# GLA value products in a new order, sums of chunk pairs in PSUM: a two-layer decoder trunk on one core

## The chip, the cores and the metric

The kernel runs on one core of one Trainium2 chip. The metric is the time of one execution in device microseconds (us), the median of several runs. Beside the runs there is one profiled execution, from which all rows below come. Instants in the text are us from the start of its span.

## The reference

A trunk of two layers on 1024 tokens of width 1024, all in fp32. Layer 0 mixes with attention and retention, layer 1 with gated linear attention (GLA, 4 heads, keys of 128, values of 256, chunks of 64 tokens). Behind each mixer stands a gated MLP of width 2816 with a causal convolution of three taps.

```
def odd_mixer(hn, w_in, w_alpha, b_alpha, out_gain, w_out):
    p = hn @ w_in
    g_q, g_k, g_v, g_r, g_a = jnp.split(p, cuts, axis=-1)
    log_alpha = jax.nn.log_sigmoid(g_a @ w_alpha + b_alpha) / GLA_GATE_TAU
    o = gla_chunked(to_heads(g_q), to_heads(g_k), to_heads(g_v), to_heads(log_alpha))
    return (from_heads(rms_norm(o, out_gain)) * jax.nn.silu(g_r)) @ w_out

def conv_ffn(hn, w_up, conv_w, conv_b, w_down):
    u, v = jnp.split(hn @ w_up, 2, axis=-1)
    uc = conv_b + conv_w[0] * up[:, 0:s] + ...        # causal, 3 taps, up is u padded
    return (jax.nn.silu(uc) * v) @ w_down

for layer in range(DEPTH):
    h = h + mixer(rms_norm(h, mix_norm_g[layer]))
    h = h + conv_ffn(rms_norm(h, ffn_norm_g[layer]), ...)
```

## The kernel before

The residual stream h lies in SBUF, transposed: 8 chunks of 128 channels by 1024 tokens. The tokens fall into two halves of 512, t1 and t2 (HALVES). Chunks c and c+4 are a pair (c = 0 to 3).

An fp32 matrix product is made of three matmuls: left and right operand are each split into a rounded part "hi" (made on ScalarE) and the rest "lo" (made on VectorE or GpSimd, as operand minus hi). One left tile times one right tile so costs three matmuls, two of them with the left hi and one with the left lo.

The projections from h work on blocks of two by two (two weight units by two chunk groups, two token halves) with seven products in place of eight, in the order 1, 2, 6, 7, 5, 4, 3. Each product runs over the four pairs, so it has 4 x 3 = 12 matmuls of 512 columns. In GLA's values the roles are turned round: h is the stationary side, and a product has 48 matmuls of 256 columns. The right operands are self.right[c][k], for pair c and product k. Those of products 1, 2 and 3 are "direct": a quarter of h times the norm's gain (ffn_direct, lines L1461 and L1462). Those of 6, 7, 5 and 4 are "mixed": sums of the quarters of h[c] and h[c + 4] (ffn_mixed in the MLPs, with the sums in L1480, L1481, L1482, L1486, L1493 and the splits in L1473 and L1474; gla_mixed in GLA, with L941, L942, L947, L955 and the splits in L927 and L928). For one pair these are five operations on VectorE for the sums and four splits, of which three have their lo on VectorE and that of product 5 on GpSimd. All of their inputs lie in SBUF; in GLA they overwrite h. The factor 1/rms of the norm is not in these operands. It comes in where a product is evicted, so that the squares of h (square_sum, L231) are summed beside the first products and norm_end makes rstd from them by a matmul.

Around the change the work stands so:

- **The end of a mixer's output projection.** The last sums of h (L459, VectorE, one PSUM operand each) come as the banks of the projection (L447 to L449) finish. Beside them VectorE and ScalarE make the right operands of pairs 0 and 1.
- **The first unit of the MLP's up projection** (ffn_up with first given). Product 1 runs over all four pairs and its copy p is taken by ScalarE (L1573); then mid() issues the mixed sums of pairs 2 and 3 and the squares of h[2], h[3], h[6], h[7]; products 2, 6 (copy p2, L1601), 7 (copy p7, L1602), 5, 4, 3 follow.
- **GLA.** gla_values(0) runs the seven products of the first half of the values, beside gla_mixed for pairs 0 and 1, then 2 and 3. Then the norm ends, decay_input makes the input of the decays, and gla_values(1) (the second half of the values) is interleaved with the decays of the heads: decay(h) runs two matmuls per token half (al, L1082) and a chain on VectorE and ScalarE (L1084 to L1102) that ends in the tiles eq and ek. These are kept for head 0 and written to DRAM for heads 1 to 3, to be read back later. gla_qk(h) makes q and k of a head: 84 matmuls (L982 to L984). It stands before the last decay for head 0, and for the others in the loop over heads, ahead of the head's attention. Attention of head 0 begins with gcb (L1179).

A scheduler places the instructions of each engine by priorities and modelled durations, so the order of the code is not the order on the engines; issue_after ties an instruction behind another. Buffers are named by tags: O and st are single PSUM tiles for sums and statistics; pj, z and T are pairs of PSUM tiles; lg and ap are pools in SBUF.

The block that a product runs in the MLP:

```
for c in range(4):
    bh, bl = self.right[c][k]
    nc.tensor.matmul(ps, hi[:, w], bh, ...)
    nc.tensor.matmul(ps, hi[:, w], bl, ...)
    nc.tensor.matmul(ps, lo[:, w], bh, ...)
```

Of the kernel before, what the change touches and what calls it, by code (L numbers as in the profile page):

```python
# [26 lines left out]
class Trunk:  # L27
# [903 lines left out]
    def gla_mixed(self, cs, h, keep=()):  # L931

        nc = self.nc
        t1, t2 = HALVES
        t = {}
        for i, c in enumerate(cs):
            ga, gb = [self.gains[:, 2 * NC + d:2 * NC + d + 1] for d in (c, c + 4)]
            x, y, z = h[c][:, t1], keep[i] if keep else h[c][:, t2], h[c + 4][:, t2]
            t[c] = x, y, z
            nc.vector.tensor_scalar(x, x, ga, None, op0=ALU.mult)  # L940
            nc.vector.scalar_tensor_tensor(y, h[c][:, t2], ga, x, op0=ALU.mult, op1=ALU.subtract)  # L941
            nc.vector.scalar_tensor_tensor(z, z, gb, y, op0=ALU.mult, op1=ALU.subtract)  # L942
            t2_hi = self.t2_hi = self.gla_split(6, c, z, nc.vector)
        yield
        for c in cs:
            x, y, z = t[c]
            nc.vector.tensor_tensor(x, z, x, op=ALU.subtract)  # L947
            self.gla_split(7, c, x, nc.vector)
        for c in cs:
            with self.tc.issue_after(t2_hi):  # L950
                self.gla_split(5, c, t[c][1], nc.gpsimd)
        for c in cs:
            z, w = t[c][2], h[c + 4][:, t1]
            gb = self.gains[:, 2 * NC + c + 4:2 * NC + c + 5]
            nc.vector.scalar_tensor_tensor(w, w, gb, z, op0=ALU.mult, op1=ALU.subtract)  # L955
            self.gla_split(4, c, w, nc.vector)
# [53 lines left out]
    def value_operands(self, hp, s):  # L1010
# [4 lines left out]
        for k, src in (("11", u[0]), ("21", v[0]), ("22", v[1]), ("12", u[1])):  # L1015
            raw[k] = self.load_weight(src[:, cs], 512)[0]
        return self.up_operands(raw, self.wp.tile([P, 512], F32, tag="wr", name="ws", bufs=6))

    def gla_values(self, s, ops, vt):
# [5 lines left out]
        def product(bank, k):  # L1025
            hi, lo = next(ops)
            start = bank not in banks
            if start:
                tag = {"x": "pj", "y": "z", "z": "T"}[bank]
                banks[bank] = [self.psum.tile([P, 512], F32, tag=tag, name="pv", bufs=2) for _ in range(2)]  # L1030
# [174 lines left out]
    def odd_mixer(self, start, dec, outs, res):  # L1205
# [6 lines left out]
        h, first, mixed, keep = start  # L1212
# [36 lines left out]
        for _ in mixed:  # L1249
            pass  # L1250
        for _ in self.gla_values(0, first, v[0]):
# [8 lines left out]
        ops = self.value_operands(0, 1)  # L1260
        ops = itertools.chain([next(ops) for _ in range(1)], ops)
        p1 = pool("gla1")
        fac = [p1.tile([P, NC], F32, name=f"fac{h}") for h in range(4)]
        for _ in self.gla_mixed((2, 3), h):
            pass
# [18 lines left out]
        work = self.gla_values(1, ops, v[0])  # L1284
        e = [None] * 4

        def decay(h):
            e[h] = self.gla_decay(h, ga, dp, fac[h])
            if h > 0:
                for i, t in enumerate(e[h]):  # L1290
                    nc.sync.dma_start(dec[2 * h - 2 + i], t)
# [17 lines left out]
        for h in range(4):  # L1309
            if h > 0:  # L1310
                e[h] = [self.ap.tile([P, T], F32, tag="ac", name="e", bufs=8) for _ in range(2)]
                for i, t in enumerate(e[h]):
                    nc.sync.dma_start(t, dec[2 * h - 2 + i])
# [137 lines left out]


# [11 lines left out]
    def ffn_mixed(self, cs, h, gi, tmp):  # L1464
# [3 lines left out]
        v = nc.vector  # L1468
        t = {}

        def split(c, k, x, engine):
            hi, lo = self.right[c][k] = self.op(self.slot[c, k])
            i = nc.scalar.copy(hi, x)  # L1473
            j = engine.tensor_tensor(lo, x, hi.bitcast(F32), op=ALU.subtract)  # L1474
            return i.ins, j.ins

        for c in cs:
            ga, gb = [self.gains[:, gi * NC + d:gi * NC + d + 1] for d in (c, c + 4)]
            x, y, z = t[c] = tmp(c)
# [573 lines left out]
```

## Time and profile before

| | |
|---|---|
| median of 3 runs | 2425.88 us (2424.42 to 2426.86) |
| the profiled execution | 2428.32 us, span 2426.5 us |
| mean granted clock of TensorE | 0.985 |
| TensorE (PE) busy | 95% of the span, 11672 matmuls |
| VectorE (DVE) busy | 66% |
| ScalarE (ACT) busy | 46% |
| GpSimd (POOL) busy | 60% |

The profiled execution lies 2.4 us above the median. A row of an engine's timeline gives the start in us, the duration, the engine, the line, the operation with out<-in and the tile's shape, how many instructions of the kind stand in a row, and in brackets how long the engine had been idle and what released it. [...] A busy share is an average over stages with different limits, so the stages around the change are read apart.

### The profile page before, as it was taken

What the parts mean: (1) busy time and instruction counts of PE and PEld (TensorE: products, weight loads), DVE (VectorE), ACT (ScalarE), POOL (GpSimd) and SP (SyncE); (2) the same over time, 40 slices, a digit from 0 to 9 for tenths busy, and PEclk for the clock granted to TensorE, in tenths of its full rate; (3) what the DMA queues carried; (4) which work ended last, traced back from release to release, by engine and by line L of the source; (5) the groups of instructions that cost most, each with busy time, mean ns of one, the idle gap of its engine ahead of it and who ended that gap; (6) DMA issues with size and microseconds to landing.
All of it is one profiled execution on the core that took longest, in us unless ns stands there. A gap on an engine that the chain in (4) does not pass through costs nothing. (4 is left out here: it accounts for less than half of the span.)

```text
span 2426.5 us, 33069 instructions
## 1 busy us (share of the span) xinstructions
PE 2310.9 (95%) x11672; PEld 1875.3 (77%) x11672; DVE 1595.9 (66%) x2301; ACT 1114.3 (46%) x2008; POOL 1452.9 (60%) x1098
## 2 busy tenths in 40 slices
PE   8999999998799999999998889998889999999999
PEld 8887886975678888887787668986668888887787
DVE  7667677479976666664339975459986666665234
ACT  6445443244565555552225555355465555553121
POOL 2322323356677777756867645657667777766774
PEclk9999999998999999999999999999999999999999
DMA  4010001112144443459843122232334334339953
GB/s 160 27 36 23 23 23 44 35 53 88 57 152 145 142 156 135 157 196 362 297 163 101 43 100 87 71 113 70 103 98 170 145 141 156 135 139 341 341 202 117
DMA packets 142118, 312.35 MB, mean 129 GB/s; under 512 B 16288, under 2 KB 16672, under 8 KB 141952
## 3 DMA queue, kind: packets, MB, share of 16 engines
q1 hardware_dynamic: 141952, 310.23, 36.5%
q8 instruction: 92, 1.51, 0.3%
q14 instruction: 74, 0.61, 0.1%
HBM read 210.55 MB, written 99.61 MB: 128 GB/s over the span
## 5 line engine op out<-in xcount | busy, mean ns | idle before, releaser
L72 POOL TENSOR_TENSOR wl<-wr,wh 128x512 fp32r<-128x512 f32 x499 | 670.3, 1347 | 460.3 <-ACT wh L70 446.6
L70 ACT CAST wh<-wr 128x512 fp32r<-128x512 f32 x536 | 330.2, 621 | 554.1 <-PE up L1564 194.1
L1563 PE MATMUL up<-op,wh 128*128 128x512 f32 x1232 | 490.3, 398 | 21.4 <-DVE h L459 10.6
L1564 PE MATMUL up<-op,wh 128*128 128x512 f32 x1232 | 489.6, 397 | 2.0 <-DVE op L1474 2.0
L1565 PE MATMUL up<-op,wl 128*128 128x512 f32 x1232 | 488.7, 397 | 0.0
L1712 DVE TENSOR_TENSOR h<-dn,h 128x512 f32<-128x512 f32 x224 | 153.7, 690 | 253.9 <-PE dn L1708 252.5
L1563 PEld LDWEIGHTS up<-op,wh 128*128 128x128 f32 x1232 | 232.6, 189 | 81.4 <-ACT wh L70 11.4
L1564 PEld LDWEIGHTS up<-op,wh 128*128 128x128 f32 x1232 | 232.6, 189 | 59.5 <-DVE op L1474 2.9
L1565 PEld LDWEIGHTS up<-op,wl 128*128 128x128 f32 x1232 | 232.6, 189 | 57.0
L1708 PE MATMUL dn<-op,wl 128*128 128x512 f32 x616 | 244.4, 397 | 5.7 <-POOL wl L72 5.7
L1707 PE MATMUL dn<-op,wh 128*128 128x512 f32 x616 | 244.0, 396 | 0.0
L1706 PE MATMUL dn<-op,wh 128*128 128x512 f32 x616 | 243.0, 396 | 0.0
L161 PE MATMUL pv<-wh,xhi 128*128 128x256 f32 x512 | 153.4, 300 | 1.3 <-ACT xhi L242 1.3
L162 PE MATMUL pv<-wl,xhi 128*128 128x256 f32 x512 | 146.1, 286 | 1.9 <-POOL wl L72 1.0
L163 PE MATMUL pv<-wh,xlo 128*128 128x256 f32 x512 | 145.2, 285 | 1.2 <-DVE xlo L243 1.0
L1708 PEld LDWEIGHTS dn<-op,wl 128*128 128x128 f32 x616 | 115.9, 188 | 35.6 <-POOL wl L72 7.5
L1706 PEld LDWEIGHTS dn<-op,wh 128*128 128x128 f32 x616 | 115.9, 188 | 29.0 <-DVE g L1569 0.4
L1707 PEld LDWEIGHTS dn<-op,wh 128*128 128x128 f32 x616 | 115.8, 188 | 28.2
L585 DVE TENSOR_TENSOR_SCAN r<-r,zeros 128x512 f32<-128x512 f32 (+3 forms) x96 | 104.1, 1086 | 24.6 <-ACT r L578 20.9
L1569 DVE TENSOR_TENSOR up<-up,p 128x512 f32<-128x512 f32 x88 | 61.5, 699 | 87.8 <-PE up L1565 87.8
L447 PE MATMUL out<-op,wh 128*128 128x512 f32 x224 | 91.0, 413 | 16.5 <-ACT op L352 8.7
L161 PEld LDWEIGHTS pv<-wh,xhi 128*128 128x128 f32 x512 | 97.9, 191 | 10.3 <-issue 7.6
(345 smaller groups left out, 5145.2 us busy)
## 6 DMA issues: line engine op xcount, KB each, us to landing
b<-put SPq DMA_DIRECT2D x154, 512.0 KB, 2.7
op<-b SPq DMA_DIRECT2D x308, 256.0 KB, 5.3
wr<-in_wup_dram SPq DMA_DIRECT2D x176, 256.0 KB, 2.6
wr<-in_wdn_dram SPq DMA_DIRECT2D x44, 256.0 KB, 4.1
wr<-in_we_v_dram SPq DMA_DIRECT2D x32, 256.0 KB, 2.8
wr<-in_wod_t_dram SPq DMA_DIRECT2D x32, 256.0 KB, 2.6
wr<-in_we_t_dram SPq DMA_DIRECT2D x24, 256.0 KB, 2.6
a<-in_wdn_dram SPq DMA_DIRECT2D x24, 256.0 KB, 3.9
```

Source lines behind the costliest of these rows:

```text
L70: self.last_hi = nc.scalar.copy(hi, x).ins
L72: self.last_lo = (engine or nc.gpsimd).tensor_tensor(lo, x, hi.bitcast(F32), op=ALU.subtract).ins
L161: nc.tensor.matmul(o, self.xhi[c][:, t], hi[:, w], start=start, stop=False, skip_group_check=True)
L162: nc.tensor.matmul(o, self.xhi[c][:, t], lo[:, w], start=False, stop=False, skip_group_check=True)
L163: nc.tensor.matmul(o, self.xlo[c][:, t], hi[:, w], start=False, stop=(c == NC - 1), skip_group_check=True)
L1563: nc.tensor.matmul(ps, hi[:, w], bh, start=(start and c == 0), stop=False, skip_group_check=True)
L1564: nc.tensor.matmul(ps, hi[:, w], bl, start=False, stop=False, skip_group_check=True)
L1565: nc.tensor.matmul(ps, lo[:, w], bh, start=False, stop=(c == 3), skip_group_check=True)
L1706: nc.tensor.matmul(ps, wh[:, w], gh, start=start, stop=False, skip_group_check=True)
L1707: nc.tensor.matmul(ps, wh[:, w], gl, start=False, stop=False, skip_group_check=True)
L1708: nc.tensor.matmul(ps, wl[:, w], gh, start=False, stop=end, skip_group_check=True)
L1712: nc.vector.tensor_tensor(h[d][:, s], ps, h[d][:, s], op=ALU.add)
```

## The change

It has four parts.

1. **The mixed sums go to PSUM.** A new function sums_psum is used in both places. ScalarE writes minus gain times one quarter of h to a PSUM tile, four operations on VectorE make the sums of products 6, 7, 5 and 4 in two PSUM tiles, and all four lo are made on VectorE. A pair has eight operations on VectorE as before (then five sums and three lo), one more on ScalarE and none on GpSimd. The tiles are O and st (for pair 3 of an MLP two of pj). h is no longer overwritten in GLA. A small constant tile gneg holds the negated gains.
2. **The first unit of an up projection** runs products 1, 2 and 7 over pairs 0 and 1 first (18 matmuls), then product 1 over 2 and 3, and so on; four left operands instead of two are made ahead. The squares of the four later chunks are issued behind copy p7 and no longer with mid().
3. **GLA's values**: products 1 and 2 of both halves (4 x 48 matmuls in place of 2 x 48) come first, in PSUM tiles of their own, and then the rest of the first half beside the mixed sums. Left operands of both halves are made ahead.
4. **GLA's heads**: after the decays of heads 0 and 1 and seven steps of the second half come q and k of head 0, the decay of head 2, q and k of head 1 and the decay of head 3, all ahead of attention. eq and ek of head 1 are not written to DRAM any more.

```
+    def sums_psum(self, x, g, banks, split):
+        nc = self.nc
+        v = nc.vector.scalar_tensor_tensor
+        a, b = banks
+        ga, gn, gb = g
+        nc.scalar.activation(a, x[1], AF.Copy, scale=gn)
+        v(b, x[3], gb, a, op0=ALU.mult, op1=ALU.add)
+        v(a, x[0], ga, b, op0=ALU.mult, op1=ALU.add)
+        yield split(6, a)
+        yield split(7, b)
+        v(b, x[3], gb, a, op0=ALU.mult, op1=ALU.subtract)
+        v(a, x[2], gb, a, op0=ALU.mult, op1=ALU.subtract)
+        split(5, b)
+        yield split(4, a)
...
-    def ffn_mixed(self, cs, h, gi, tmp):
+    def ffn_mixed(self, cs, h, gi, banks):
...
-            v.tensor_scalar(x, h[c][:, t1], ga, None, op0=ALU.mult)
-            v.scalar_tensor_tensor(y, h[c][:, t2], ga, x, op0=ALU.mult, op1=ALU.subtract)
-            v.scalar_tensor_tensor(z, h[c + 4][:, t2], gb, y, op0=ALU.mult, op1=ALU.subtract)
-            split(c, 6, z, v)
...
-            v.tensor_tensor(x, z, x, op=ALU.subtract)
-            split(c, 7, x, v)
...
-            split(c, 5, t[c][1], nc.gpsimd)
...
-            v.scalar_tensor_tensor(z, h[c + 4][:, t1], gb, z, op0=ALU.mult, op1=ALU.subtract)
-            last = split(c, 4, z, v)
...
+            sums.append(self.sums_psum(x, g, banks(c), functools.partial(split, c)))
+        for _ in range(3):
+            last = [next(x) for x in sums][-1]
...
-        x = product("x", 1)
+        late = range(4)
+        if first is not None:
+            late = (2, 3)
+            product("x", 1, (0, 1))
+            product("y", 2, (0, 1))
+            lefts[6] = next(ops)
+            product("z", 7, (0, 1))
+        x = product("x", 1, late)
         nc.scalar.copy(p, x)
         if first is not None:
             mid()
-        y = product("y", 2)
+        y = product("y", 2, late)
...
         nc.scalar.copy(p2, product("x", 6))
-        nc.scalar.copy(p7, product("z", 7))
+        i = nc.scalar.copy(p7, product("z", 7, late))
+        if first is not None:
+            with self.tc.issue_after(i.ins):
+                squares()
...
-        for _ in self.gla_values(0, first, v[0]):
+        works = [self.gla_values(s, firsts[s], v[0], (("pj", "z", "z"), ("T", "z", "z"))[s]) for s in range(2)]
+        for work in works:
+            next(work)
+            next(work)
+        for _ in itertools.chain(*mixed[:2]):
+            pass
+        for _ in itertools.islice(works[0], 2):
+            pass
+        for _ in itertools.chain(*mixed[2:]):
+            pass
+        for _ in works[0]:
             pass
...
-        step(3)
+        step(1)
         decay(0)
-        step(4)
+        step(2)
         decay(1)
-        step(2)
-        decay(2)
         step(7)
         self.gla_qk(0, *e[0], p1, s2())
+        decay(2)
+        self.gla_qk(1, *e[1], p1, s2())
         decay(3)
```

The order on the engines, at three places. VectorE at the end of layer 1's output projection, before (out and h in L459 are the projection's sums, bt the temporary tiles of the mixed sums, op the operands):

```order
L459 TENSOR_TENSOR h<-out,h 128x512
L1493 SCALAR_TENSOR_TENSOR bt<-h,gains,bt 128x512
L1462 SCALAR_TENSOR_TENSOR op<-h,gains,op 128x512 x2
L459 TENSOR_TENSOR h<-out,h 128x512
L1474 TENSOR_TENSOR op<-bt,op 128x512
L1462 SCALAR_TENSOR_TENSOR op<-h,gains,op 128x512 x2
L459 TENSOR_TENSOR h<-out,h 128x512
L1480 TENSOR_SCALAR bt<-h,gains 128x512
L1462 SCALAR_TENSOR_TENSOR op<-h,gains,op 128x512
L459 TENSOR_TENSOR h<-out,h 128x512
```

and after (mx are the PSUM tiles of the sums; L1480 is now the lo of the direct operands, L1490 that of the mixed ones):

```order
L459 TENSOR_TENSOR h<-out,h 128x512
L1465 SCALAR_TENSOR_TENSOR mx<-h,gains,mx 128x512
L1466 SCALAR_TENSOR_TENSOR mx<-h,gains,mx 128x512
L1490 TENSOR_TENSOR op<-mx,op 128x512
L459 TENSOR_TENSOR h<-out,h 128x512
L1490 TENSOR_TENSOR op<-mx,op 128x512
L1480 SCALAR_TENSOR_TENSOR op<-h,gains,op 128x512 x2
L459 TENSOR_TENSOR h<-out,h 128x512
```

The sums of h stand among the same kinds of work, which now read one SBUF tile and one PSUM tile each.

ScalarE in the first unit of layer 1's up projection, before (p is the copy of product 1, p_16556 and p_16557 are p2 and p7, nsq the squares):

```order
L1573 COPY p<-up 128x512
L1473 CAST op<-bt 128x512 x3
L70 CAST wh<-wr 128x512
L1473 CAST op<-bt 128x512
L231 ACTIVATE nsq<-h 128x512 x6
L1601 COPY p_16556<-up 128x512
L231 ACTIVATE nsq<-h 128x512 x2
L1602 COPY p_16557<-up 128x512
L257 CAST shi<-ssum 128x512
```

and after (L1591, L1619 and L1620 are the copies p, p2 and p7):

```order
L1591 COPY p<-up 128x512
L1489 CAST op<-mx 128x512
L70 CAST wh<-wr 128x512 x2
L1489 CAST op<-mx 128x512
L70 CAST wh<-wr 128x512
L1489 CAST op<-mx 128x512
L1619 COPY p_16549<-up 128x512
L1620 COPY p_16550<-up 128x512
L231 ACTIVATE nsq<-h 128x512 x8
L257 CAST shi<-ssum 128x512 x2
```

The copies p2 and p7 moved ahead of all eight squares.

VectorE at the entry of GLA, before (L1712 are the last sums of h, gv the values that are evicted from pv):

```order
L1712 TENSOR_TENSOR h<-dn,h 128x512 x3
L941 SCALAR_TENSOR_TENSOR y<-h,gains 128x512 x2
L942 SCALAR_TENSOR_TENSOR h<-h,gains,y 128x512 x2
L947 TENSOR_TENSOR h<-h 128x512
L928 TENSOR_TENSOR op<-h,op 128x512 x3
L947 TENSOR_TENSOR h<-h 128x512
L955 SCALAR_TENSOR_TENSOR h<-h,gains 128x512 x2
L928 TENSOR_TENSOR op<-h,op 128x512 x3
```

and after:

```order
L1733 TENSOR_TENSOR h<-dn,h 128x512 x3
L1461 SCALAR_TENSOR_TENSOR mx<-h,gains,mx 128x512
L232 TENSOR_TENSOR ssum<-ssum,nsq 128x512
L1462 SCALAR_TENSOR_TENSOR mx<-h,gains,mx 128x512
L232 TENSOR_TENSOR ssum<-ssum,nsq 128x512
L1046 TENSOR_TENSOR gv<-pv,gv 128x2x256
L938 TENSOR_TENSOR op<-mx,op 128x512
L1046 TENSOR_TENSOR gv<-pv,gv 128x2x256
```

The sums come one pair at a time now, with squares and evictions between them. On TensorE, 229 of GLA's 336 matmuls of values of 256 columns stand ahead of the first decay matmul (al) before; after, 300 of them do, with 7 matmuls of head 0's q and k.

## Rows read from the trace of the kernel before

**Rows 1.** The page: the span, then TensorE's busy time.

```profile
span 2426.5 us, 33069 instructions
PE 2310.9 (95%) x11672; PEld 1875.3 (77%) x11672; DVE 1595.9 (66%) x2301; ACT 1114.3 (46%) x2008; POOL 1452.9 (60%) x1098
```

**Rows 2.** TensorE's timeline at the start of layer 0's MLP: waits.

```profile
637.09 0.47 PE L447 MATMUL out<-op,wh 128*128 128x512 f32 x1 [2.04 <-DVE h L459]
...
645.42 0.76 PE L1563 MATMUL up<-op,wh 128*128 128x512 f32 x1 [5.30 <-DVE h L459]
...
665.24 0.50 PE L1563 MATMUL up<-op,wh 128*128 128x512 f32 x1 [3.34 <-ACT p L1601]
```

**Rows 3.** The same of layer 1's MLP.

```profile
1741.27 0.47 PE L447 MATMUL out<-op,wh 128*128 128x512 f32 x1 [1.54 <-ACT op L1473]
...
1745.26 0.47 PE L447 MATMUL out<-op,wh 128*128 128x512 f32 x1 [0.98 <-DVE h L459]
...
1750.34 0.47 PE L447 MATMUL out<-op,wh 128*128 128x512 f32 x1 [2.04 <-DVE h L459]
...
1758.66 0.77 PE L1563 MATMUL up<-op,wh 128*128 128x512 f32 x1 [5.30 <-DVE h L459]
...
1767.32 0.51 PE L1563 MATMUL up<-op,wh 128*128 128x512 f32 x1 [1.14 <-ACT p L1573]
...
1770.92 0.50 PE L1564 MATMUL up<-op,wh 128*128 128x512 f32 x1 [1.00 <-DVE op L1474]
...
1778.47 0.50 PE L1563 MATMUL up<-op,wh 128*128 128x512 f32 x1 [3.31 <-ACT p L1601]
```

**Rows 4.** By stage: busy us of each engine, granted clock, DMA share, GB/s.

```profile
1758.60:1762.30 3.70, 3.64 (x9) 2.89 (x10) 3.63 (x4) 1.82 (x4) 2.37 (x3) 0.50 0.43 143
1762.60:1774.70 12.10, 9.96 (x42) 7.43 (x41) 12.02 (x13) 5.06 (x10) 8.94 (x6) 1.00 0.22 66
...
1778.50:1785.70 7.20, 7.20 (x24) 5.71 (x25) 4.82 (x6) 4.14 (x8) 4.64 (x4) 0.76 0.01 3
1306.90:1339.90 33.00, 23.52 (x170) 22.28 (x169) 33.00 (x36) 18.10 (x34) 25.16 (x18) 0.90 0.25 82
1339.90:1362.40 22.50, 17.64 (x98) 11.55 (x96) 22.29 (x28) 11.86 (x22) 13.25 (x9) 0.92 0.17 56
1362.40:1404.60 42.20, 37.57 (x202) 31.40 (x203) 38.21 (x51) 24.13 (x43) 30.44 (x22) 0.96 0.18 62
```

**Rows 5.** VectorE's groups, 600 to 662 us: busy us, mean ns; last row: the page.

```profile
L1474 DVE TENSOR_TENSOR op<-bt,op 128x512 fp32r<-128x512 f32 x12 | 11.4, 973 | 0.1
L459 DVE TENSOR_TENSOR h<-out,h 128x512 f32<-128x512 f32 x14 | 9.5, 680 | 0.2 <-PE out L449 0.2
...
L1486 DVE TENSOR_TENSOR bt<-bt 128x512 f32<-128x512 f32 x4 | 5.9, 1484 | 0.1
L1493 DVE SCALAR_TENSOR_TENSOR bt<-h,gains,bt 128x512 f32<-128x512 f32 x4 | 5.5, 1363 | 0.0
L1481 DVE SCALAR_TENSOR_TENSOR bt<-h,gains,bt 128x512 f32<-128x512 f32 x4 | 4.3, 1075 | 0.1
L1482 DVE SCALAR_TENSOR_TENSOR bt<-h,gains,bt 128x512 f32<-128x512 f32 x4 | 4.0, 1006 | 0.0
...
L1569 DVE TENSOR_TENSOR up<-up,p 128x512 f32<-128x512 f32 x88 | 61.5, 699 | 87.8 <-PE up L1565 87.8
```

**Rows 6.** ScalarE's timeline, layer 1's first unit: six squares in a row.

```profile
1774.33 3.62 ACT L231 ACTIVATE nsq<-h 128x512 f32<-128x512 f32 x6
```

**Rows 7.** TensorE's timeline in GLA: the first matmuls of decays, and attention's first.

```profile
1362.44 0.47 PE L1082 MATMUL al<-ga,walpha 96*128 96x512 f32 x1 [0.93 <-DVE ga L1246]
...
1381.58 0.50 PE L1082 MATMUL al<-ga,walpha 96*128 96x512 f32 x1 [1.19 <-DVE eq L1102]
...
1395.56 0.49 PE L1082 MATMUL al<-ga,walpha 96*128 96x512 f32 x1 [3.22 <-DVE eq L1102]
...
1424.67 1.19 PE L1179 MATMUL gcb<-gv,gkt 128*128 128x256 f32 x2 [5.03 <-DVE eq L1102]
```

More of the change, by code (lines that the diff above doesn't have):

```diff
@@ L929, in gla_split, with gla_mixed, split @@
         return i.ins
-    def gla_mixed(self, cs, h, keep=()):
-        nc = self.nc
+    def gla_mixed(self, c, h):
         t1, t2 = HALVES
[L935 to L956, printed above, removed]
+        def split(k, x):
+            hi, lo = self.right[c][k] = self.op(self.slot[c, k])
+            i = self.nc.scalar.copy(hi, x).ins
+            self.nc.vector.tensor_tensor(lo, x, hi.bitcast(F32), op=ALU.subtract)
+            if k == 6:
+                self.t2_hi = i
+        d = 2 * NC + c
+        g = self.gains[:, d:d + 1], self.gneg[:, 4 + c:5 + c], self.gains[:, d + 4:d + 5]
+        x = h[c][:, t1], h[c][:, t2], h[c + 4][:, t1], h[c + 4][:, t2]
+        return self.sums_psum(x, g, (self.stat("mx", "O"), self.stat("mx", "st")), split)
     def pair_raw(self, u, v):
@@ L1210, in pool @@
             return tc.alloc_tile_pool(name=name, bufs=1, side=side, reuse_waits="tile")
-        h, first, mixed, keep = start
+        h, firsts, mixed, keep = start
         def decay_input():
@@ L1534, in put, with ffn_up @@
         nc.sync.dma_start(self.bsp[j // 2][k], t.bitcast(F32))
-    def ffn_up(self, layer, j, pools, first=None, mid=None, stats=None):
+    def ffn_up(self, layer, j, pools, first=None, mid=None, squares=None, stats=None):
         nc = self.nc
@@ L1551, in ffn_up, with product @@
         banks = {}
-        def product(bank, k):
-            hi, lo = next(ops)
+        lefts = {}
+        def product(bank, k, cs=range(4)):
+            if k not in lefts:
+                lefts[k] = next(ops)
+            hi, lo = lefts[k]
             start = bank not in banks
@@ L1559, in product @@
             ps = banks[bank]
-            for c in range(4):
+            for c in cs:
                 bh, bl = self.right[c][k]
@@ L1768, in layer @@
         ops = self.up_operands(self.up_weights(layer, 0), s2)
-        ops = itertools.chain([next(ops) for _ in range(2)], ops)
+        ops = itertools.chain([next(ops) for _ in range(4)], ops)
         self.norm_begin(self.lg, 3, ("glo", "glo", "glo"))
@@ L1772, in layer, with banks @@
             [self.lg.tile([P, 512], F32, tag="glo", name="nsq", bufs=3)]
[L1774 removed]
+        def banks(c):
             if c < 3:
[L1776 to L1777 removed]
+                return self.stat("mx", "O"), self.stat("mx", "st")
+            return self.pj("mx"), self.pj("mx")
         for c in range(2):
@@ L1788, in layer, with squares @@
                 self.ffn_direct(c, k, h, gi)
-        def mid():
-            with contextlib.ExitStack() as st:
-                for i in self.ffn_mixed((2, 3), h, gi, tmp):
-                    st.enter_context(tc.issue_after(i))
-                for d in (2, 3, 6, 7):
-                    self.square_sum(h[d])
-        first = [ops, mid, lambda: self.norm_end(False, "pj")]
+        def squares():
+            for d in (2, 3, 6, 7):
+                self.square_sum(h[d])
+        first = [ops, lambda: self.ffn_mixed((2, 3), h, gi, banks), squares, lambda: self.norm_end(False, "pj")]
         self.nup = 0
@@ L1873, in layer, with get @@
             return
-        ops = self.value_operands(0, 0)
-        first = itertools.chain([next(ops) for _ in range(3)], ops)
-        self.vp = pool("vp", "right")
-        keep = pool("keep")
-        mixed = self.gla_mixed((0, 1), h, [self.lg.tile([P, 512], F32, tag="ghi", name="y", bufs=3),
-                                           keep.tile([P, 512], F32, name="y")])
-        next(mixed)
-        return h, first, mixed, keep
+        keep = pool("keep")
+        def get(k):
+            return self.lg.tile([P, 512], F32, tag="ghi", name="wr", bufs=3) if k == "21" else \
+                keep.tile([P, 512], F32, name="ws")
+        ops = [self.value_operands(0, 0, get), self.value_operands(0, 1)]
+        made = [[next(o) for _ in range(2)] for o in ops]
+        made[0] += [next(ops[0]) for _ in range(2)]
+        self.vp = pool("vp", "right")
+        mixed = [self.gla_mixed(c, h) for c in range(4)]
+        next(mixed[0])
+        return h, [itertools.chain(m, o) for m, o in zip(made, ops)], mixed, keep
     def run(self):
```

62 lines of the change are left out of this document (28 added, 34 removed).

## The prediction

> **What bounds the kernel now.** I read the page first: TensorE is busy for 2310.9 of 2426.5 us [rows 1], so its chain is the bound and only two things can be won: time in which TensorE waits, and time in which it runs at the lower clock. Next I went through TensorE's timeline for its waits, and kept those in the stages that the change touches. Layer 0's MLP begins after waits of 2.04 and 5.30 us for VectorE's sums of h, and its first unit stops for 3.34 us at a copy of ScalarE [rows 2]. Layer 1's MLP shows the same picture, complete in the rows: 1.54, 0.98, 2.04 and 5.30 us up to the first matmul, then 1.14, 1.00 and 3.31 us inside the first unit [rows 3]. In GLA the waits are spread out; there the table by stage says more. From 1306.9 to 1362.4 us, up to the first decay matmul, VectorE is busy for 55.3 of 55.5 us and TensorE for 41.2 [rows 4]: VectorE is the bound of that stage. From there to attention each head's decay starts about 14 us after the one before (1381.58, 1395.56) and TensorE stands for 0.93, 1.19, 3.22 and, before attention, 5.03 us, nearly all for the chain's last operation on VectorE [rows 7].
>
> The lower clock: in the 3.70 us after the wait of 5.30 us the granted clock is 0.50, and 9 matmuls take 3.64 us; later, at 1.00, 42 take 9.96 us, or 0.237 us each [rows 4]. So about 1.5 us are lost there. After the wait of 3.31 us the clock is 0.76 on average and 24 matmuls take 7.20 us in place of 5.7 [rows 4]: again 1.5 us. I price a lost low stretch at 1.5 us each time.
>
> **The change part by part.**
>
> **Sums in PSUM, at the two tails.** Ahead of an MLP VectorE has no pause, and the last sums of h, for which TensorE waits, stand in its queue among operand work. For four pairs of layer 0 that work is 11.4 + 5.9 + 5.5 + 4.3 + 4.0 = 31.1 us (I leave out three short multiplications), 7.8 us a pair. These operations have both inputs in SBUF and take 973 to 1484 ns on average. One with an input in PSUM takes 680 ns (the sums of h), and one whose result goes back to PSUM as well 699 ns [rows 5]. The new form has eight of those a pair: 8 x 0.69 = 5.5 us, though the lo of product 5 is now among them. That is 2.3 us less a pair. Two pairs are made ahead of the start, so 4.6 us a layer leave VectorE's queue in front of the last sums. I take all of it off the waits, which are 7.3 us in layer 0 and 9.9 us in layer 1 [rows 2, 3]: 9.2 us. Bounds: nothing, if the queue fills up with other work that was waiting; 17.2 us, if the waits go altogether. The shorter last wait should spare the low stretch behind it: 2 x 1.5 = 3.0 us (0 to 3.0). What ScalarE gains in work, one activation a pair, is 0.6 us by the squares' rate of 3.62 us for six [rows 6], and lies beside VectorE's work; if that cover is gone it delays the first sum of a pair by as much.
>
> [...] The rows say that a PSUM input makes an operation of this size cheaper here, 680 against 973 ns or more [rows 5]. [...]
>
> **The first unit of the up projections.** It starts with 18 matmuls on pairs 0 and 1, 18 x 0.237 = 4.3 us of work for which pairs 2 and 3 needn't be ready. That covers the two waits of about 1 us for their operands [rows 3]. The wait of 3.31 us is for copy p2, which stands on ScalarE behind six squares, 3.62 us [rows 3, 6]; after the change both copies stand ahead of all squares. The wait goes, and nothing on TensorE is behind the squares until the norm's matmul. What is late next is the norm: its squares start later, so rstd comes closer to its first use; I leave 0.4 us a layer for that. Layer 1's three waits are 5.45 us; for layer 0 I take the same two small ones and its 3.34 us, 5.5 us. Gain 10.9 - 0.8 = 10.1 us (bounds 5 to 10.9), and the two low stretches after the long wait, 3.0 us (0 to 3.0).
>
> **GLA, from its entry to attention.** The values' first products need only direct operands. With those of both halves first, 48 more matmuls lie beside the mixed sums. VectorE saves 4 x 2.3 = 9.2 us of sums and takes in the evictions of half 1, 8 x 0.68 = 5.4 us, so the first decay matmul moves from 1362.4 to about 1358.6. From there to attention VectorE's chain now takes 1424.7 - 1362.4 = 62.2 us [rows 7]. To it come the evictions and products for head 1's q and k, eight operations, 5.4 us; VectorE has 4.0 us of 42.2 free in the first part of that stretch [rows 4], so I let half of them fit in: 2.7 us. Attention then starts at 1358.6 + 62.2 + 2.7 = 1423.5, 1.2 us sooner than now, with head 1's 84 matmuls done, 84 x 0.237 = 19.9 us. Together 21 us; I take 20. A check from TensorE's side: its idle time is 14.3 us up to the first decay matmul [rows 4] and over 10 us from there to attention [rows 7], and the clock's means of 0.90 to 0.96 [rows 4] cost some 6 us, so 30 us is the ceiling and 20 fits under it. Lower bound 8 us: the entry no shorter, and all of the added operations, with a few waits, in the chain. The upper bound is 28. The tiles of head 1 that stay in SBUF take two writes and two reads off the DMA queue; its share is 0.18 there [rows 4], and nothing waits for it: no term.
>
> **What is new to pay.** The chain ScalarE, VectorE, ScalarE in two PSUM tiles that a pair must share; GLA's product banks, each freed by an eviction that now stands behind sums; h read later by the sums, so that its buffers come free later. No row shows these. The nearest ones are the waits of about 1 us for a single operand [rows 3]. I take four of them, 4 us (bounds 0, since the order gives TensorE other work at each place, to 12).
>
> **The sum.** 9.2 + 3.0 + 10.1 + 3.0 + 20 - 4 = 41.3 us. From the profiled execution, 2428.3 - 41.3 = 2387.0 us. This execution lies 2.4 us over the median of the runs, so the median is 2384.6; I say 2385.
>
> **The rivals.**
>
> *VectorE's queue stays full.* The order shows VectorE as dense ahead of the MLPs as before. If what was saved is filled with operands of the next pairs, the wait of 5.30 us stays: the tails then give 2.3 us in place of 9.2 and no clock, GLA 16, and the new waits cost 6. 2.3 + 10.1 + 3.0 + 16 - 6 = 25.4 us: 2403 profiled, 2400 as a median. For it speaks that these waits are for VectorE and not for its operations on sums alone; against it that less work stands ahead of the last sums. Chance 0.25, between 2396 and 2412.
>
> *An operation on sums in PSUM is dearer than its row.* The 699 ns are from an operation with another second input [rows 5]. Halfway to the 973 ns of the old lo it would be 0.84 us, 1.2 us more a pair, and over the eight pairs that lie in front of something 10 us: 2395. [...] Chance 0.06.
>
> *Slower: the two tiles make the sums serial.* A pair is one activation, two sums, two splits, two sums, two splits on two engines in turn. Strictly in turn that is 5 x 0.6 on ScalarE [rows 6] + 5.5 us = 8.5 us, hardly over the 7.8 of now. If each hand-over added enough to make it 12 us, the twelve pairs would lose 12 x 4.2 = 50 us, and what the new orders give by themselves (10.1 + 3.0 + about 10 in GLA) would not make up for it: 2428 + 27 = 2455, a median of 2453. It decides from about 9.7 us a pair. Against it: the code keeps two pairs or other work between the steps, so the engines don't wait in turn. Chance 0.05.
>
> *More goes than I count:* the tails' waits vanish and GLA gives 28 us, without new waits: 2362. Chance 0.04. That the change doesn't do what it says I exclude: the order shows the copies, the sums and the matmuls of both halves at their new places.
>
> **How the numbers follow.** The forecast, 2372 to 2396, has 0.60; with the rivals 0.25, 0.06, 0.05 and 0.04. The range for 8 in 10 runs from 2366 to 2406: it leaves out the slower case, the better one and the far end of the full queue. A measurement of this kernel tells about 0.2%, 5 us, from no change. All but the serial case and the end of the first rival are faster by more: faster 0.92, within 0.2% 0.03, slower 0.05.
>
> **What would show it right or wrong.** In the changed kernel's trace: the last wait before each MLP's first matmul at 3 us or less in place of 5.30 and the clock at 1.00 soon after; no wait of over 1 us at the copies p2 and p7; operations with mx near 0.7 us; the first decay matmul within 53 us of the entry; attention's first matmul about where it was with head 1's q and k ahead of it. I am wrong if mx operations take 0.9 us or more, if VectorE's queue leaves the 5.30 us as they are, if new waits of several us stand at GLA's product banks, or if attention of head 0, without head 1's matmuls between its steps, stops TensorE more than before.

## The result and the profile after

The changed kernel takes 2382.22 us, the median of 4 runs (2380.29 to 2384.88), against 2426.37 us before in the same comparison: a ratio of 0.982, 95% interval 0.9803 to 0.9837. That is 44 us faster, 3 us under the forecast of 2385 and well inside the range. The profiled execution took 2383.14 us, 45.2 us less than that of before.

The page of the changed kernel, the two lines that answer to [rows 1]: as many matmuls, in a span that is 45 us shorter.

```profile
span 2381.4 us, 33055 instructions
PE 2298.3 (97%) x11672; PEld 1869.9 (79%) x11672; DVE 1551.2 (65%) x2302; ACT 1119.2 (47%) x2020; POOL 1426.6 (60%) x1086
```

Where the time went is read from the instants at which TensorE starts each stage. Each length below is the difference of two such instants in the timeline of one profiled execution, in us; "after" is the changed kernel, and the other columns are experiments of the next section.

| stage, from first matmul to first matmul | before | after | sb_ffn | w21_wr | best_split |
|---|---|---|---|---|---|
| output projection 0 to up projection 0 | 104.8 | 96.6 | 104.8 | 96.6 | 96.6 |
| up projection 0 to down projection 0 | 443.0 | 441.6 | 443.3 | 436.9 | 437.9 |
| GLA's values to output projection 1 | 341.3 | 320.4 | 322.0 | 322.2 | 321.6 |
| output projection 1 to up projection 1 | 110.4 | 100.4 | 110.8 | 101.0 | 101.4 |
| up projection 1 to down projection 1 | 443.0 | 440.4 | 442.4 | 437.1 | 436.4 |

So the two tails (the output projections of the mixers, from their first matmul to the MLP's) gave 8.2 + 10.0 = 18.2 us, the two up projections 1.4 + 2.6 = 4.0 us, and GLA 20.9 us. What is left of the 45.2 us lies in stages that the change doesn't touch, 2 us over the whole span; one of them, from down projection 1 to the end, takes 221.7 to 225.1 us in the fourteen profiled executions of this study, so a difference of 2 or 3 us in one stage of one execution says little.

TensorE's timeline at the start of the MLPs, the rows that answer to [rows 2, 3]. The columns are start, duration, instruction, and in brackets the idle time before it with what ended it:

```profile
664.19 0.50 PE L1573 MATMUL up<-op,wh 128*128 128x512 f32 x1 [3.17 <-ACT wh L70]
...
667.22 0.79 PE L1575 MATMUL up<-op,wl 128*128 128x512 f32 x1 [2.29 <-POOL wl L72]
...
1717.20 0.47 PE L1573 MATMUL up<-op,wh 128*128 128x512 f32 x1 [0.49 <-DVE h L459]
...
1744.16 0.49 PE L1573 MATMUL up<-op,wh 128*128 128x512 f32 x1 [2.52 <-ACT wh L70]
...
1747.19 0.80 PE L1575 MATMUL up<-op,wl 128*128 128x512 f32 x1 [2.23 <-POOL wl L72]
```

Of the waits of [rows 2, 3], 0.49 us is left ahead of layer 1's first unit, where it was 5.30, and 0.40 us in each layer for copy p; the others are gone. One wait for h early in layer 1's output projection grew from 0.82 to 2.38 us. And each layer has two new waits that stood in no row of before, for the left operands of the second unit: 5.5 us in layer 0 and 4.75 us in layer 1.

The table by stage, with the columns of [rows 4] (busy time of PE, PEld, DVE, ACT and POOL, granted clock of TensorE as a share of full speed, DMA share, GB/s). The first row is the start of layer 1's MLP, the second the stretch with the new waits, and the last three are GLA from its entry to the first decay matmul, then to attention in two pieces:

```profile
1717.20:1722.20 5.00, 5.00 (x21) 3.92 (x22) 4.29 (x7) 2.79 (x5) 1.68 (x2) 1.00 0.50 159
...
1741.60:1752.00 10.40, 5.65 (x15) 4.15 (x15) 5.63 (x10) 5.88 (x9) 10.32 (x9) 0.67 0.27 89
...
1296.40:1355.10 58.70, 49.81 (x344) 42.98 (x343) 50.33 (x73) 33.93 (x61) 41.01 (x30) 0.94 0.19 64
1355.10:1397.30 42.20, 40.78 (x187) 32.35 (x188) 37.73 (x55) 27.64 (x51) 34.14 (x23) 1.00 0.16 50
1397.30:1412.60 15.30, 14.60 (x71) 11.72 (x71) 11.98 (x20) 9.31 (x18) 11.70 (x9) 1.00 0.40 139
```

The first unit starts at a granted clock of 1.00 (0.50 before, [rows 4]); in the later stretch with the new waits it is 0.67 on average. GLA's entry takes 58.7 us now, longer than the 55.5 of before, with 344 matmuls in it in place of 266. TensorE is busy for 55.4 of the 57.5 us from there to attention.

VectorE's groups from 600 to 662 us, which answer to [rows 5] (busy us, mean ns, idle before):

```profile
L1480 DVE SCALAR_TENSOR_TENSOR op<-h,gains,op 128x512 fp32r<-128x512 f32 x12 | 11.8, 998 | 1.0 <-ACT op L1479 1.0
L1490 DVE TENSOR_TENSOR op<-mx,op 128x512 fp32r<-128x512 f32 x16 | 10.5, 682 | 0.1
...
L1462 DVE SCALAR_TENSOR_TENSOR mx<-h,gains,mx 128x512 f32<-128x512 f32 x4 | 3.0, 751 | 0.0
```

The other three sums are within 4 ns of the one shown. A pair costs 4 x 0.75 + 4 x 0.682 = 5.7 us on VectorE (5.5 forecast, 7.8 before).

### The profile page after: what moved, and what is told of

Same layout as the page of the kernel before. It is cut to its first block, busy times and chain, and to the rows that moved or that the text cites. A ratio compares the mean times of both kernels' runs of the same rounds, so it can differ in the third digit from the quotient of the medians.

```text
span 2381.4 us, 33055 instructions
## 1 busy us (share of the span) xinstructions
PE 2298.3 (97%) x11672; PEld 1869.9 (79%) x11672; DVE 1551.2 (65%) x2302; ACT 1119.2 (47%) x2020; POOL 1426.6 (60%) x1086
## 5 line engine op out<-in xcount | busy, mean ns | idle before, releaser
L72 POOL TENSOR_TENSOR wl<-wr,wh 128x512 fp32r<-128x512 f32 x499 | 665.6, 1338 | 448.8 <-ACT wh L70 423.2
```

The costliest lines, as they stand in the source:

```text
L72: self.last_lo = (engine or nc.gpsimd).tensor_tensor(lo, x, hi.bitcast(F32), op=ALU.subtract).ins
```

## The experiments

Every median below is set beside that of the kernel before in its own comparison (2425.5 to 2427.7 us).

**One half of the change at a time.** ffn_only is the kernel before with the MLPs' part alone, gla_only with GLA's part alone.

> The kernel before with the MLPs' part of the change alone (sums in PSUM there, products 1, 2 and 7 on pairs 0 and 1 first, squares behind copy p7, the second unit's load); GLA as before. Theory (the parts add up): the instants of the two traces give 18.2 us at the two tails and 4.0 us in the two first units, so 2426 - 22 = 2404 us (2401 to 2407). Rival (the stages help each other, as by an earlier GLA entry): off by more than 5 us from that.

> The kernel before with GLA's part of the change alone (sums in PSUM there, products 1 and 2 of both halves first, head 1's q and k ahead of attention); the MLPs as before. Theory (the parts add up): the instants of the two traces give 20.9 us from GLA's first matmul to its output projection, so 2426 - 21 = 2405 us (2402 to 2408). Rival: with layer 1's MLP as before, its tail gives some of it back, 2410 us or more.

ffn_only: 2402.54 us, ratio 0.9902 (0.9888 to 0.9917). gla_only: 2407.23 us, ratio 0.9921 (0.9906 to 0.9936). Against 2427.53 us these are 25.0 and 20.3 us, together 45.3: the parts add up, and neither leans on the other.

**The tails: sums back in SBUF.** sb_ffn is the changed kernel with the MLPs' sums as before. The edit, in short:

```
-            sums.append(self.sums_psum(x, g, banks(c), functools.partial(split, c)))
+            x, y, z = t[c] = tmp(c)
+            v.tensor_scalar(x, h[c][:, t1], ga, None, op0=ALU.mult)
+            v.scalar_tensor_tensor(y, h[c][:, t2], ga, x, op0=ALU.mult, op1=ALU.subtract)
...
```

> The changed kernel with the MLPs' mixed sums back in SBUF (operations and tiles as before, lo of product 5 on GpSimd); the second unit's weight tile goes back to the ring with it, since the sums need its place. Theory (the sums' cost on VectorE is what TensorE waits for at the tails): waits of 7 us and more per layer come back ahead of the first unit, and some for pairs 2 and 3 in it, so 2382 + 18 = 2400 us (2396 to 2406). Rival (the new order of the first unit removed the tails' waits, since it needs less at its start): tails without waits, 2380 to 2388 us.

2405.13 us, ratio 0.9909 (0.9894 to 0.9925): 23 us of the gain are lost with this part alone by the medians, 20 by the profiled executions. TensorE's timeline in sb_ffn:

```profile
634.11 0.47 PE L447 MATMUL out<-op,wh 128*128 128x512 f32 x1 [2.06 <-DVE h L459]
642.44 0.77 PE L1585 MATMUL up<-op,wh 128*128 128x512 f32 x1 [5.30 <-DVE h L459]
...
1736.62 0.76 PE L1585 MATMUL up<-op,wh 128*128 128x512 f32 x1 [3.73 <-DVE h L459]
```

The waits for the last sums of h are back, 5.30 us to the hundredth in layer 0, and both tails have the lengths of before in the table. The new order of the first unit is there all the same and removes nothing of them. So the tails' whole gain comes from the sums in PSUM, with the lo of product 5 that moved from GpSimd to VectorE beside them; no run parts these two.

**The first unit without the 18 matmuls ahead.** nopairs drops this part:

```
-            late = (2, 3)
-            product("x", 1, (0, 1))
-            product("y", 2, (0, 1))
-            lefts[6] = next(ops)
-            product("z", 7, (0, 1))
```

> The changed kernel with one part undone: the first unit runs its products over all four pairs at once, without the 18 matmuls on pairs 0 and 1 first. Theory (those 18 matmuls, 4.3 us, cover the operands of pairs 2 and 3): waits of 2 to 5 us a layer appear in the first unit, so 2386 to 2392 us. Rival (with the sums in PSUM the operands are in time anyway): 2380 to 2385 us.

2384.77 us, ratio 0.9827 (0.9812 to 0.9842), 2.5 us over the changed kernel, within the spread of the runs: the rival's answer. The first unit has no wait for operands of pairs 2 and 3; with the sums in PSUM they are in time, and the order adds little.

**The squares' place.** sq_mid puts the squares back with the mixed sums, ahead of the copies p2 and p7.

> The changed kernel with one part undone: the squares of the four later chunks are issued with the mixed sums, ahead of the copies p2 and p7, as in the kernel before. Theory (the copies stood behind the squares on ScalarE): the wait of 3.3 us comes back in both layers with the lower clock behind it, up to 2 x (3.3 + 1.5) = 9.6 us, and the waits that the late norm causes go, so 2388 us (2385 to 2392). Rival (the late squares cost as much through the norm and VectorE's queue as they save): 2379 to 2384 us.

2378.33 us, ratio 0.9806 (0.9786 to 0.9826). My theory falls: undoing this part does not make the kernel slower (its runs, 2374.82 to 2382.72 us, overlap those of the changed kernel from below). TensorE's timeline in sq_mid, layer 1:

```profile
1733.23 0.50 PE L1573 MATMUL up<-op,wh 128*128 128x512 f32 x1 [2.70 <-ACT p L1620]
```

The wait behind the squares does come back, 2.70 us. But the two waits for the second unit's operands, 4.75 us, are gone. The move had bought one with the other.

**The new waits.** GpSimd makes the second unit's operands, and the changed kernel's timeline of GpSimd shows it idle for 11 us until a weight has landed; the waits of the DMA queue that SyncE feeds tell why (total, times, longest):

```profile
1740.82 1.29 POOL L1523 TENSOR_TENSOR wr<-wr 128x512 f32<-128x512 f32 x1 [10.99 <-DMA wr<-in_wup_dram]
```

```profile
SPq L1512 <- DVE slo L258: 9.7, 1, 9.7
```

The load is tile "21" of the second unit. The change gives it a tile in another pool, an edit that its description does not list. On SyncE the request, issued at 1737.79 us and landed at 1740.75, waits for no operation of an engine; yet ahead of it stands a load of the third unit that waits 9.7 us, until the norm has used a tile (slo, L258). So the late squares, by way of the norm, hold a weight. Two kernels take this away: w21_wr undoes the change of tile, w21_early requests the load ahead of the norm.

```
-            if j > {"21": 0, "22": 1}.get(k, NF):
+            if k in ("21", "22") and j > 1:
```

> The changed kernel with one part undone: the weight tile "21" of the second unit is loaded into the ring of six weight tiles, as in the kernel before, and not into the third pool. Theory (the queue's order, above): the two waits go here as well, about 2370 us (2367 to 2374). Rival (the ring is what was short, and the undone edit was made for it): the loads of the second unit come later for want of a tile, the waits stay or grow, 2380 to 2390 us.

> The changed kernel, with one load moved: the weight tile "21" of the second unit of each up projection is requested ahead of the norm, in the same SBUF tile, so that it no longer stands on the DMA queue behind a load of the third unit that waits for the norm's last operation on VectorE (9.7 us on the queue). Theory (the queue's order makes the two new waits at the second unit's left operands, 3.2 + 2.3 us in layer 0, 2.5 + 2.2 us in layer 1): both waits go, with the lower clock behind them, 5 to 7 us a layer, so about 2382 - 12 = 2370 us (2367 to 2373). Rival (GpSimd's chain of four operations of 1.27 us each, or another of the unit's loads, is as late): waits of 2 us or more stay, 2378 to 2383 us.

w21_wr: 2379.58 us, ratio 0.9805 (0.9788 to 0.9821). w21_early: 2381.67 us, ratio 0.9812 (0.9797 to 0.9826). In both the waits for the second unit's operands are gone, so the queue was their cause; but the medians moved by 0.5 and 2.6 us and not by 12. The table shows more for w21_wr: its two up projections are 8.0 us shorter than those of the changed kernel, in a profiled execution that was the fastest of its four. So the gain lies between 3 and 8 us, and these runs don't fix it better. TensorE's timeline in w21_wr, layer 1, and VectorE's ahead of it:

```profile
1735.17 0.50 PE L1573 MATMUL up<-op,wh 128*128 128x512 f32 x1 [1.93 <-DVE v L1579]
1737.95 0.50 PE L260 MATMUL pn<-slo,ones_d 128*128 128x512 f32 x1 [0.58 <-DVE slo L258]
1742.14 0.49 PE L1573 MATMUL up<-op,wh 128*128 128x512 f32 x1 [0.67 <-ACT p L1591]
```

```profile
1728.01 6.50 DVE L232 TENSOR_TENSOR ssum<-ssum,nsq 128x512 f32<-128x512 f32 x7 [1.62 <-ACT nsq L231]
1734.43 0.69 DVE L1579 TENSOR_TENSOR v<-up,p 128x512 f32<-128x512 f32 x1
```

What was next late is the late squares themselves: seven of VectorE's additions of squares, 6.50 us, stand ahead of the sum v that frees a bank of TensorE. That is 3.2 us of new waits for 4.75 of old ones in layer 1. In w21_early the up projections are shorter too, by 4.2 and 3.5 us, but the tails are 1.8 and 2.9 us longer, with a wait of 1.69 us for h at layer 1's first matmul. The weight is there so early that GpSimd works on the second unit beside the tail (its operation s<-wr below, which comes behind the tail in the changed kernel), and VectorE's twelve direct lo, whose two inputs both lie in SBUF, take 13.7 us there in place of 11.5 (first row: the changed kernel; the others: w21_early):

```profile
L1480 DVE SCALAR_TENSOR_TENSOR op<-h,gains,op 128x512 fp32r<-128x512 f32 x12 | 11.5, 979 | 0.8 <-ACT op L1479 0.8
...
L1480 DVE SCALAR_TENSOR_TENSOR op<-h,gains,op 128x512 fp32r<-128x512 f32 x12 | 13.7, 1160 | 1.1 <-ACT op L1479 1.1
...
1716.81 1.63 POOL L1527 TENSOR_TENSOR s<-wr 128x512 f32<-128x512 f32 x1
...
1721.88 0.47 PE L1576 MATMUL up<-op,wh 128*128 128x512 f32 x1 [1.69 <-DVE h L459]
```

**Squares in two parts.** If early squares hold ScalarE's copies and late ones VectorE's sums, each should hold neither when halved. best_split is w21_wr with the squares of h[2] and h[3] beside the mixed sums and those of h[6] and h[7] behind p7; best_p2 has all eight between p2 and p7.

```
+                for d in (2, 3):
+                    self.square_sum(h[d])
         def squares():
-            for d in (2, 3, 6, 7):
+            for d in (6, 7):
                 self.square_sum(h[d])
```

> The changed kernel with the second unit's weight tile back in the ring, and with the squares split: h[2] and h[3] with the mixed sums, h[6] and h[7] behind copy p7. Theory (both orders of the squares cost about 3 us a layer, early ones by holding the copies on ScalarE, late ones by holding VectorE's sums and the norm): with four on each side neither wait is over 1 us, so 4 to 8 us under the changed kernel: 2375 us (2372 to 2379). Rival (each half is still long enough to hold its engine): 2378 to 2383 us.

> The same with all eight squares between the copies p2 and p7. Theory (p7 is not needed before product 4, some 5 us after p2): no wait at the copies, the norm 2.8 us sooner than in the changed kernel, 2375 us (2372 to 2380). Rival (p7 stands behind 4.5 us of squares and holds the sum of product 5): a wait of 1 to 3 us for it, 2378 to 2384 us.

> The changed kernel once more, for a comparison on the same chip: 2382 us (2380 to 2385).

best_split: 2377.44 us (2376.13 to 2380.24), ratio 0.9794 (0.9777 to 0.9811). best_p2: 2378.17 us (2376.87 to 2381.33), ratio 0.9794. The changed kernel beside them: 2383.68 us (2382.52 to 2387.79), ratio 0.9821. The runs of best_split and of the changed kernel do not overlap, so it is the faster one by some 6 us. But it differs from the changed kernel in two edits, the weight's tile and the split, and w21_wr has the first alone: its median is 2.1 us higher, its runs (2376.83 to 2380.78 us) overlap those of best_split, and its two up projections are as long (874.0 us, 874.3 in best_split). So what the split adds by itself is not shown. In best_split's timeline two waits of over 1 us are left in layer 1's first unit:

```profile
1737.82 0.49 PE L260 MATMUL pn<-slo,ones_d 128*128 128x512 f32 x1 [1.14 <-DVE slo L258]
1743.94 0.50 PE L1573 MATMUL up<-op,wh 128*128 128x512 f32 x1 [1.01 <-ACT p L1591]
```

Against best_p2 it is not told apart (0.7 us); there TensorE waits 1.85 us for copy p7, as its rival said. Nor is it told apart from sq_mid (2378.33 us).

**GLA, part by part.** heads_old is the changed kernel with head 1's q and k behind attention of head 0, as before. gla_psum is the kernel before with nothing but GLA's sums in PSUM.

```
-        decay(2)
-        self.gla_qk(1, *e[1], p1, s2())
+        decay(2)
...
-            if h > 1:
+            if h > 0:
```

> The changed kernel with one part undone: head 1's q and k go back behind attention of head 0, and its eq and ek through DRAM; the values' order and the sums in PSUM stay. Theory (head 1's 84 matmuls fill the time in which the decays' chain on VectorE holds TensorE): waits of 8 to 12 us come back ahead of attention, so 2390 to 2396 us. Rival (the values' order alone gave GLA's 21 us): 2380 to 2386 us.

> The kernel before with GLA's mixed sums in PSUM, pair by pair, and nothing else: the values' order, the heads' order and the MLPs as before. Theory (VectorE is the bound from GLA's entry to the first decay matmul, and the sums in PSUM relieve it by some 9 us): the first decay matmul comes 5 to 9 us sooner, 2417 to 2422 us. Rival (what GLA gains at its entry comes from the values' order, whose matmuls fill TensorE's waits): 2423 to 2427 us.

heads_old: 2398.87 us, ratio 0.9884 (0.9869 to 0.9898), 3 us over the range of my theory and far from the rival's: this part is worth some 16 us (16.7 by the medians of two comparisons, 15.6 in the table below). gla_psum: 2428.29 us, ratio 1.0 (0.9991 to 1.0009): nothing. The stage from GLA's first matmul to the output projection, from the four timelines, in us:

| | to the first decay matmul | on to attention | on to the projection | sum |
|---|---|---|---|---|
| before | 55.5 | 62.2 | 223.6 | 341.3 |
| gla_psum: sums in PSUM | 62.9 | 58.3 | 224.4 | 345.7 |
| heads_old: and the values' order, decay of head 2 later | 59.4 | 53.5 | 223.1 | 336.0 |
| after: and head 1 ahead | 58.7 | 57.5 | 204.2 | 320.4 |

TensorE's timeline in heads_old, the first matmul of the last head's decay and attention's first:

```profile
1398.74 0.50 PE L1077 MATMUL al<-ga,walpha 96*128 96x512 f32 x1 [2.03 <-DVE eq L1097]
...
1410.03 1.19 PE L1174 MATMUL gcb<-gv,gkt 128*128 128x256 f32 x2 [10.09 <-DVE eq L1097]
```

From gla_psum to heads_old two things change in GLA, the values' order and the place of head 2's decay, which now comes behind q and k of head 0; heads_old has the MLPs' part as well. Without head 1's matmuls TensorE stands for 10.09 us ahead of attention; with them, in the changed kernel, for 0.72 us:

```profile
1412.62 0.67 PE L1174 MATMUL gcb<-gv,gkt 128*128 128x256 f32 x2 [0.72 <-DVE eq L1097]
```

The table by stage of gla_psum, its entry, and the waits of VectorE in the entry of the changed kernel (total, times, longest):

```profile
1306.50:1369.40 62.90, 45.96 (x276) 38.26 (x275) 48.12 (x69) 31.68 (x57) 28.18 (x21) 0.81 0.18 59
```

```profile
DVE op L938 <- ACT op L937: 3.7, 4, 1.4
DVE mx L1461 <- ACT mx L1460: 3.3, 3, 1.5
```

VectorE is relieved in both: it is busy for 48.1 of 62.9 us in gla_psum and for 50.3 of 58.7 in the changed kernel, where it was busy for 55.3 of 55.5 us before [rows 4]. But in the changed kernel it now waits 7.0 us for ScalarE, in an order in which the sums of all four pairs go one after another through the same two PSUM tiles. That these two tiles make the entry longer is not shown: in gla_psum, where it is longest, VectorE waits for ScalarE's part of the sums only 2.8 us, and 7.4 us for TensorE. There TensorE is idle for 16.9 us (14.3 before) and busy for 4.8 us longer, with ten more matmuls and at a granted clock of 0.81 (0.91 before). No run gives GLA's sums more tiles. That the total of gla_psum shows nothing of the 4.4 us by which GLA is longer is within what the stages vary: its last stage, which is the same code, was 3.2 us shorter in that profile. I take from it that the sums in PSUM bring GLA nothing by themselves; what they bring beside the new values' order, no run shows.

## Why the prediction was right, and where its steps were not

By the stages of the table, in us of one profiled execution each:

| step | forecast | measured |
|---|---|---|
| tails' waits, two layers | 9.2 | 18.2 |
| first units, with the low stretches after the tails' and the unit's long wait | 10.1 + 3.0 + 3.0 | 4.0 |
| GLA to its output projection | 20 | 20.9 |
| new waits | -4 | in the rows above |
| elsewhere | 0 | 2 |
| sum | 41.3 | 45.2 |

The time was right, GLA's sum too, and two errors of some 10 us cancelled: that the forecast came within 3 us is luck to that extent.

**The tails were sized at half.** The mechanism held in outline: VectorE's queue ahead of the last sums was what TensorE waited for, as sb_ffn shows (5.30 and 3.73 us ahead of the first units; none in layer 0 and 0.49 us in layer 1 in the changed kernel), and the sums in PSUM shortened it. My term was 2.3 us a pair and 4.6 us a layer. In layer 0's tail VectorE's mixed operations took 17.2 us before and 11.4 after, in layer 1's 18.8 and 11.4: 5.8 and 7.4 us. Besides, operations that the change does not touch became shorter, the direct lo by 1.0 and 1.2 us and the lo of the weights (L72) by 1.0 and 0.6, which I had at nothing. Together 7.8 and 9.2 us, near the 8.2 and 10.0 us by which the tails became shorter. The upper bound, that the waits go altogether, was the right value. VectorE and GpSimd in layer 0's tail by stage, before and after, over the same work (third and fifth busy time):

```profile
600.00:645.40 45.40, 37.81 (x161) 29.51 (x160) 43.70 (x51) 23.40 (x39) 26.04 (x17) 0.97 0.14 47
...
599.40:636.60 37.20, 37.20 (x161) 29.83 (x160) 35.97 (x50) 23.78 (x41) 20.61 (x14) 1.00 0.17 58
```

Why these operations were dear I had read too simply. I took 973 ns and more as the price of an operation with both inputs in SBUF. These means mix two prices. In the trace of the kernel before, the old split (L1474) took 676 to 684 ns each of the eight times that no GpSimd operation ran beside it, and 1120 ns on average, up to 1785, the sixteen times that one did; the sums of h, with one input in PSUM, took 675 to 692 ns either way. Four rows of VectorE and the four of GpSimd that go with them, in layer 0's first unit:

```profile
647.17 1.80 DVE L1486 TENSOR_TENSOR bt<-bt 128x512 f32<-128x512 f32 x1
648.89 0.68 DVE L459 TENSOR_TENSOR h<-out,h 128x512 f32<-128x512 f32 x1
...
655.25 1.78 DVE L1486 TENSOR_TENSOR bt<-bt 128x512 f32<-128x512 f32 x1
656.95 1.88 DVE L1474 TENSOR_TENSOR op<-bt,op 128x512 fp32r<-128x512 f32 x3
```

```profile
647.14 1.28 POOL L1474 TENSOR_TENSOR op<-bt,op 128x512 fp32r<-128x512 f32 x1 [1.34 <-ACT op L1473]
648.38 1.74 POOL L1518 TENSOR_TENSOR s<-wr 128x512 f32<-128x512 f32 x1
...
654.73 1.75 POOL L72 TENSOR_TENSOR wl<-wr,wh 128x512 fp32r<-128x512 f32 x1
658.28 1.71 POOL L72 TENSOR_TENSOR wl<-wr,wh 128x512 fp32r<-128x512 f32 x1 [1.80 <-ACT wh L70]
```

So what PSUM bought was not a cheaper operation: the old sums of two tiles in SBUF took 692 to 752 ns in the kernel before where no GpSimd operation ran beside them. It bought one that takes no longer beside GpSimd: in the tails and first units of the changed kernel the sums in PSUM took 740 to 756 ns each and their splits 674 to 692, with a GpSimd operation beside them or without. That fits the lo that became shorter without being touched, since GpSimd has 5 us less to do in layer 0's tail (20.6 us in place of 26.0), and w21_early, where it has more to do beside layer 1's tail and the direct lo become longer (13.7 us in place of 11.5). No run takes GpSimd's work away altogether.

**The first units failed by an edit that I did not cost.** I wrote that nothing on TensorE is behind the squares until the norm's matmul, and left 0.4 us a layer. Behind the norm stood a DMA request on SyncE's queue, and behind that a weight of the second unit, which the change had moved to that pool. I had asked what the squares hold up on ScalarE's queue, and not what waits for the norm on SyncE's. With that mended, VectorE's queue was next: the additions of the squares. sq_mid shows that moving the squares was worth nothing in the end: it cost what it gave, or more.

**The 18 matmuls ahead** were to cover two waits of about 1 us a layer. nopairs shows that the sums in PSUM would have made these operands in time without them.

**GLA came out right by wrong steps.** The entry was to be 3.8 us shorter, because VectorE had less to do; it is 3.2 us longer, and my sign of 53 us to the first decay matmul failed with 58.7. I had named a mechanism, the two tiles that make the sums serial, as the rival for the slower side, and gave it 0.05 with the remark that other work stands between the steps. In the changed kernel's entry VectorE does wait for ScalarE, 7.0 us; whether that is what makes the entry longer stays open, as said above. What pays is order. More matmuls of the values fill the entry (344 matmuls, 266 before); from gla_psum to heads_old GLA becomes 9.7 us shorter, with the later decay of head 2 in it. And head 1's 84 matmuls, of which 72 run ahead of attention's first, fill the wait for the decays' chain, 15.6 us. Attention starts 116.2 us after GLA's first matmul, where it was 117.7 before, and 1.2 us sooner was forecast: the longer entry and a shorter way from there (57.5 us in place of the 64.9 that I had counted) made up for each other. From there to the output projection GLA is 19.4 us shorter, near the 19.9 us that I had taken for the 84 matmuls.

**Slips in what stands above.** A product of GLA's values has 24 matmuls and not 48: four blocks of tokens, two pairs, three matmuls. The 336 matmuls are the fourteen products of both halves, and the products 1 and 2 of both halves are 4 x 24. A half is a half of the sum: gla_values(0) runs over pairs 0 and 1, and gla_values(1) adds pairs 2 and 3. The 48 more matmuls of the prediction are right. The rival on the better side adds up to about 2364 by its own terms, and not to 2362. The first two heads' decays start 19 us apart, only the later ones 14. No step hangs on these.

**The rivals.** VectorE's queue did not stay full. An operation on sums in PSUM took 747 to 751 ns on average and its split 682, near the row that I had taken, and not 0.84 us. Nor does an input in PSUM show as dearer where GpSimd stands still: in the kernel before, with no GpSimd operation beside them, the sums of h with one input in PSUM took 676 to 692 ns and the old split with both in SBUF 676 to 684.

## What to carry to other kernels

When a step is moved later, follow what waits for its result through every queue, the one that feeds DMAs included: a request that waited for a buffer held the one behind it here for 9.7 us, and a weight that was free to come was as late as the buffer. Split a mean before you call it the price of an operation: the 973 ns of VectorE's old split were 680 ns alone and 1120 ns beside GpSimd. In GLA an order that puts work of one engine under another's chain was worth 25 us, and cheaper operations alone nothing; in the tails, where VectorE's queue was what TensorE waited for, they were worth 18 us. And a wait that goes is worth what the next late thing leaves of it: with each place of the squares other waits of 2 to 5 us a layer appeared, and sq_mid, w21_wr, best_split and best_p2 end within 2.2 us of one another.

## What the runs showed that I had not expected

A load that waited for no operation of any engine stood still for 9.7 us behind another one's wait on SyncE. VectorE's old split, with both inputs in SBUF, took 0.68 us with GpSimd idle and up to 1.8 us with GpSimd busy beside it, and the sums of h, with one input in PSUM, 0.68 us in both cases. And in GLA's entry VectorE was busy for 5 us less than before and waited 7 us for ScalarE, and the entry was 3.2 us longer.
